# A hybrid convolution and retention layer on one core: an early pool for the first pair, other engines and places for small steps

## The chip, the core and the metric

The kernel runs on one core of a Trainium2 chip. Its engines work side by side, each through its own row of instructions: TensorE (PE; its weight loads are PEld), VectorE (DVE), ScalarE (ACT), GpSimd (POOL) and SyncE (SP), which here issues most transfers. Transfers can also be issued from ScalarE's and GpSimd's rows. The metric is device time in microseconds, the median of several runs; lower is better. All data are fp32.

## The reference

One decoder layer for x of 1024 positions by 1024 channels. A conditioned RMS norm gives u; one projection gives the parts of a convolution branch (gated a, a causal depthwise convolution over 31 positions, a layer norm, a 1024 by 1024 product, a gate) and of a retention branch with 4 heads (q and k with a rotary turn, chunks, a head norm, a gate). Both go through one output projection, a gated residual and a last RMS norm.

```python
u = _rmsnorm(h, norm_g[l]) * (1.0 + scale) + shift
proj = u @ w_in[l]          # conv a, b, gate; q, k, v; ret gate
a = conv_a * jax.nn.sigmoid(conv_bp)
a = _causal_depthwise_conv(a, conv_w[l], conv_b[l])
a = jax.nn.silu(_layernorm(a, conv_ln_g[l], conv_ln_b[l]))
y_conv = (a @ conv_pw[l]) * jax.nn.silu(conv_gate)
r = _retention_chunkwise(_rotary(q), _rotary(k) * RET_QK_DIM ** -0.5, v)
y_ret = _head_groupnorm(r, ...) * jax.nn.silu(ret_gate)
h = h + gate * (jnp.concatenate([y_conv, y_ret], axis=-1) @ w_out[l])
return _rmsnorm(h, final_g)
```

## The kernel before

**Three matmuls for one.** Every fp32 operand is split into a high part (a cast on ScalarE) and a low part (the operand less its high part, on VectorE or GpSimd); `split` (L69 to 71) does both, and `mm3` (L81 to 84) multiplies high by high, low by high and high by low. A low part is an instruction with two operands in SBUF.

**Stages in order of time.** `head` (L145 to 258) norms and turns x and projects the first four units of 128 output channels (tiles ps_e, ps_pcc, ps_paa, ps_pdd), step by step over eight blocks of the inner dimension; `make_u` (L206) gives uh and ul of a block, `mod` (L193, tile junk) the conditioning, `wel` (L166) the weights' low part. At its end the weights of the two *plain* units (22 and 23) are split (`hi_s`, `lo_s`, L256). Then the plain units run (L330), and beside them the sums of quarters of u for the pairs (L317 to 319, tile xs) and their splits th and tl.

**Pairs.** The other projection units go two by two, 21 pairs, each with seven block products in place of eight: blocks 11, 12, 21, 22 of a pair's weights are loaded (tiles pr), added and subtracted on GpSimd (s1 to s4; tiles sm and pr, L383), and split (ph on ScalarE L377, pl on GpSimd L378). `operands` (L368) does this, `pair` (L455) multiplies into the PSUM tiles pa, pd and pb. While a pair runs, VectorE does the convolution's taps of earlier channels (`conv_taps`, L260): 30 instructions at L271 for each of eight groups of 128 channels, in PSUM (yp) or, for the last group, in SBUF (y). At the end of each group GpSimd adds it to ysum (L278).

**Values, retention and norm.** The first half of the values (tiles ps_v, vs; L498 to 517) follows the pairs. `retention` (L585) then does heads 0 to 3, four chunks each (a tile of head 2, chunk 1 has 21 in its name): loads of q, k, sg, v, their splits (qch, qcl, kch, kcl, vch, vcl), scores sp, sm, outputs op and ob, the state, a norm (rs on GpSimd, nb on VectorE, rn on ScalarE, tp on TensorE), and a store of the gated result to d_yr (L691). `values` (L574) does the second half of the values among heads 0 and 1. `ln_squares` (L535) takes the mean over channels with two matmuls of ysum (tiles mu, negmu), subtracts it from eight loaded groups (ys, L546), stores these again and adds up their squares (L553). `ln_scale` (L555) makes the scale from that sum, `norm_z` the normed groups, `pointwise` (L714) the 1024 by 1024 product.

**Output.** `load_r` (L741) loads and splits blocks of the output weights (wo, woh, wol), which are multiplied with the stored halves d_yr and d_yc.

**What sets the order.** A scheduler writes each engine's row ahead of time from the order of the program, its priorities and modelled times; on the chip an engine takes its row in that order and waits where an operand isn't ready. Tiles come from pools; a place in a pool is used again when its last reader is done, and pools opened one after another take the memory of those closed before.

```python
        for tag, dt, bufs in (("raw", F32, 6), ("sum", F32, 3), ("ph", F32R, 7), ("pl", F32R, 7)):
            op_.tile([P, HK, P], dt, tag=tag, name=f"first_{tag}", bufs=bufs)
```

## Time and profile before

| | us |
|---|---|
| median of three runs | 982.46 (981.14 to 988.12) |
| profiled execution, its time | 983.87 |
| its span, first to last instruction | 982.1 |
| TensorE busy | 942.8 |
| VectorE busy | 742.7 |
| ScalarE busy | 410.4 |
| GpSimd busy | 395.6 |
| mean granted clock of TensorE | 0.984 |

Durations in the profile are those of the one profiled execution, and times in it count from the span's start. The granted clock is a share of full speed. An engine that shows little busy time can still be what another waits for; such waits stand in brackets in the timelines, with the instruction that ended them.

### The profile page before, as it was taken

The page shows a single profiled execution, that of the slowest core. Times are in us where ns is not written, and L with a number is a line of the kernel's source. Part 1 is how long each engine was busy: PE and PEld are TensorE (multiplying, and loading weights), DVE is VectorE, ACT ScalarE, POOL GpSimd, SP SyncE. Part 2 cuts the span into 40 slices and gives each one's busy share as a digit, 9 for nine tenths or more (in the row PEclk, how much of TensorE's full clock was granted, in tenths as well). Part 3 has the DMA queues.
Part 4 walks back from the last instruction along what each step waited for, and adds up shares of the span by engine and source line. Part 5 has one row for each costly group of instructions (what it writes and reads, how often), then busy time and mean ns, then how long its engine had stood idle before and what let it go on. Part 6 is the DMA issues. An engine that isn't in the chain of part 4 may idle for free.

```text
span 982.1 us, 12550 instructions
## 1 busy us (share of the span) xinstructions
PE 942.8 (96%) x4496; PEld 786.4 (80%) x4496; DVE 742.7 (76%) x926; ACT 410.4 (42%) x676; POOL 395.6 (40%) x356
## 2 busy tenths in 40 slices
PE   6999999999999999999999899979998999999996
PEld 5877788888888888888888788868887876888886
DVE  6989989898999999999799747788874354522322
ACT  7755543424334334343431556577543233311201
POOL 3021998878978878897561111212111000000000
PEclk9999999999999999999999899989999999999999
DMA  9912333324343334443344757875974386432111
GB/s 352 328 58 69 114 119 135 111 86 125 112 128 130 128 108 140 132 147 105 145 134 152 272 163 261 313 240 179 326 231 150 108 288 220 150 113 86 64 43 44
DMA packets 85441, 154.95 MB, mean 158 GB/s; under 512 B 6657, under 2 KB 44289, under 8 KB 84098
## 3 DMA queue, kind: packets, MB, share of 16 engines
q1 hardware_dynamic: 83074, 148.12, 44.9%
q10 hardware_dynamic: 1584, 3.41, 0.9%
q0 software_dynamic: 720, 2.62, 0.7%
q8 instruction: 35, 0.57, 0.2%
q14 instruction: 28, 0.23, 0.1%
HBM read 107.99 MB, written 46.14 MB: 157 GB/s over the span
## 4 chain that ended last, share of the span: by engine, by line
PE 79%; DMA 8%; DVE 5%; issue 3%; ACT 2%; POOL 1%; SPq 0%; POOLq 0%; DVEq 0%; ACTq 0%
PE pa L84 8%; PE pa L83 8%; PE pa L82 8%; PE ps_o L83 4%; PE ps_o L84 4%; PE ps_o L82 4%; PE pb L84 4%; PE pb L82 4%; PE pb L83 4%; DMA wo<-w_out 3%; PE ps_v L82 2%; PE ps_v L83 2%; PE ps_v L84 2%; PE pd L82 2%; PE pd L84 2%
## 5 line engine op out<-in xcount | busy, mean ns | idle before, releaser
L271 DVE SCALAR_TENSOR_TENSOR yp<-a,vec_t,yp 128x1024 f32<-128x1024 f32 x210 | 269.6, 1284 | 15.0 <-ACT yp L269 11.1
L378 POOL TENSOR_TENSOR pl<-pr,ph 128x512 fp32r<-128x512 f32 x63 | 83.8, 1336 | 70.9 <-ACT ph L377 70.5
L378 POOL TENSOR_TENSOR pl_s<-sm_s,ph_s 128x512 fp32r<-128x512 f32 x63 | 83.3, 1326 | 25.3 <-ACT ph_s L377 21.3
L675 POOL TENSOR_TENSOR rs<-mv,kc_t 128x2 f32<-128x2 f32 x16 | 6.3, 394 | 187.9 <-DVE mv L672 176.6
L377 ACT CAST ph_s<-sm_s 128x512 fp32r<-128x512 f32 x63 | 39.0, 622 | 99.9 <-PE pa L83 95.1
L790 POOL TENSOR_TENSOR fr<-fr,mhalf 128x1 f32<-128x1 f32 x7 | 3.8, 545 | 177.6 <-DVE fr L789 177.6
L377 ACT CAST ph<-pr 128x512 fp32r<-128x512 f32 x63 | 38.7, 621 | 75.9 <-PE pa L83 31.4
L82 PE MATMUL pa<-th,ph_s 128*128 128x512 f32 x168 | 65.5, 390 | 1.0 <-ACT ph_s L377 1.0
L84 PE MATMUL pa<-th,pl_s 128*128 128x512 f32 x168 | 65.5, 390 | 0.7 <-POOL pl_s L378 0.7
L82 PE MATMUL pb<-uh,ph_s 128*128 128x512 f32 x168 | 65.4, 389 | 0.0
L83 PE MATMUL pa<-tl,ph_s 128*128 128x512 f32 x168 | 65.4, 389 | 0.0
L83 PE MATMUL pb<-ul,ph_s 128*128 128x512 f32 x168 | 65.4, 389 | 0.0
L84 PE MATMUL pb<-uh,pl_s 128*128 128x512 f32 x168 | 65.4, 389 | 0.0
L383 POOL TENSOR_TENSOR sm_s<-pr,pr 128x512 f32<-128x512 f32 x42 | 55.7, 1326 | 5.2 <-PE pa L84 1.8
L83 PE MATMUL ps_pw<-zl,hi_pw 128*128 128x512 f32 x128 | 50.8, 397 | 1.1 <-DVE zl L71 1.1
L84 PE MATMUL ps_pw<-zh,lo_pw 128*128 128x512 f32 x128 | 50.3, 393 | 0.0
L271 DVE SCALAR_TENSOR_TENSOR y<-a,vec_t,y 128x1024 f32<-128x1024 f32 x30 | 44.4, 1480 | 6.6 <-ACT y L269 5.8
L82 PE MATMUL ps_pw<-zh,hi_pw 128*128 128x512 f32 x128 | 48.6, 404 | 0.0
L781 DVE TENSOR_TENSOR g<-ps_o,gate 128x512 f32<-128x512 f32 x14 | 9.5, 690 | 49.3 <-PE ps_o L84 49.3
L83 PE MATMUL ps_o<-wol,hi_yr 128*128 128x512 f32 x112 | 44.6, 398 | 0.1
L84 PE MATMUL ps_o<-woh,lo_yr 128*128 128x512 f32 x112 | 44.1, 396 | 0.0
L83 PE MATMUL ps_o<-wol,hi_yc 128*128 128x512 f32 x112 | 44.0, 393 | 0.1
(446 smaller groups left out, 2800.5 us busy)
## 6 DMA issues: line engine op xcount, KB each, us to landing
pr<-w_p SPq DMA_DIRECT2D x84, 256.0 KB, 2.8
aw<-ada_ss SPq DMA_DIRECT2D x8, 1024.0 KB, 7.5
d_qk<-ro SPq DMA_DIRECT2D x16, 512.0 KB, 3.3
wo<-w_out SPq DMA_DIRECT2D x16, 512.0 KB, 4.4
xt<-x SPq DMA_DIRECT2D x8, 512.0 KB, 6.8
d_sg<-o SPq DMA_DIRECT2D x16, 256.0 KB, 2.1
sg<-d_sg SPq DMA_DIRECT2D x16, 256.0 KB, 4.0
v<-d_v SPq DMA_DIRECT2D x16, 256.0 KB, 3.9
```

What stands on the lines that cost most here:

```text
L82: nc.tensor.matmul(ps, lh, rh, start=start, stop=False, skip_group_check=more)
L83: nc.tensor.matmul(ps, lh, rl, start=False, stop=False, skip_group_check=more)
L84: nc.tensor.matmul(ps, ll, rh, start=False, stop=stop, skip_group_check=more)
L271: nc.vector.scalar_tensor_tensor(acc, ap[:, j:j + S], col(V_CW, m * CW + j), acc, op0=MUL, op1=ADD)
L377: nc.scalar.copy(hi, src)
L378: nc.gpsimd.tensor_tensor(lo, src, hi.bitcast(F32), op=SUB)
L383: nc.gpsimd.tensor_tensor(out, a, b, op=op)
L675: nc.gpsimd.tensor_tensor(rs, mv[:, :, 1], kc_t[:, K_G2 + 2 * h:K_G2 + 2 * h + 2], op=MUL)
L781: nc.vector.tensor_tensor(g[:, :n], ps(), gate[:, sl], op=MUL)
L790: nc.gpsimd.tensor_tensor(r, r, mhalf[:, 0:1], op=ALU.pow)
```

## The change

Five things. The low parts of the plain units' weights are made on VectorE. A small pool, `early`, is opened ahead of the pool of th and tl, in memory that the head has used; the first pair's loads, the splits of its blocks 11 and 12 and its sums are written ahead of the plain units and live there, as the raw blocks of all pairs do; the parts of 11 and 12 get rings of two places, the others of five, where all shared rings of seven. `ln_squares` is written ahead of the second values of head 0 and no longer behind them. The stores of d_yr in the last head are issued from GpSimd's row. And the tags of the retention pool are placed in another order: mask, q, k, v, sg, vch and vcl first, ktl last.

```diff
@@ -253,7 +253,7 @@
         for j, n in enumerate(STD):
             hi = sw.tile([P, KT, P], F32R, tag="hi", name=f"hi_s{n}")
             lo = sw.tile([P, KT, P], F32R, tag="lo", name=f"lo_s{n}")
-            split(hi, lo, raw[:, j].rearrange("p (k c) -> p k c", k=KT), nc.gpsimd)
+            split(hi, lo, raw[:, j].rearrange("p (k c) -> p k c", k=KT))
             ws.append((hi, lo))
         return ps, ws
 
@@ -307,6 +307,10 @@
 
 
     one_ctx = ctx.enter_context(ExitStack())
+    early_p = one_ctx.enter_context(tc.tile_pool(name="early", bufs=1, reuse_waits="tile"))
+    pools = {"a": early_p}
+    for tag, dt, bufs in (("rawa", F32, 3), ("rawb", F32, 3), ("sum", F32, 3), ("pha", F32R, 2), ("pla", F32R, 2)):
+        early_p.tile([P, HK, P], dt, tag=tag, name=f"first_{tag}", bufs=bufs)
     tpool = one_ctx.enter_context(tc.tile_pool(name="t", bufs=1, reuse_waits="tile"))
     th = {i: tpool.tile([P, HK, HALF], F32R, name=f"th{i}") for i in (2, 3, 4)}
     tl = {i: tpool.tile([P, HK, HALF], F32R, name=f"tl{i}") for i in (2, 3, 4)}
@@ -321,6 +325,38 @@
         split(th[3][:, k], tl[3][:, k], x12)
         split(th[4][:, k], tl[4][:, k], x21)
 
+    def parts(pools, src, p, n):
+
+        tag, bufs = ("a", 2) if n in ("11", "12") else ("b", 5)
+        hi = pools[tag].tile([P, HK, P], F32R, tag="ph" + tag, name=f"ph{p}_{n}", bufs=bufs)
+        lo = pools[tag].tile([P, HK, P], F32R, tag="pl" + tag, name=f"pl{p}_{n}", bufs=bufs)
+        nc.scalar.copy(hi, src)
+        nc.gpsimd.tensor_tensor(lo, src, hi.bitcast(F32), op=SUB)
+        return hi, lo
+
+    def blocks(p, pools):
+
+        raw = {}
+        for i, b in enumerate(("11", "12", "21", "22")):
+            raw[b] = early_p.tile([P, HK, P], F32, tag="rawa" if i < 2 else "rawb", name=f"pr{p}_{b}", bufs=3)
+            nc.sync.dma_start(raw[b], w_p[p, i])
+
+        def sum_(n, a, b, op, out=None):
+            out = early_p.tile([P, HK, P], F32, tag="sum", name=f"sm{p}_{n}", bufs=3) if out is None else out
+            nc.gpsimd.tensor_tensor(out, a, b, op=op)
+            return out
+
+        o = {"11": parts(pools, raw["11"], p, "11"), "12": parts(pools, raw["12"], p, "12")}
+        s3 = sum_("s3", raw["11"], raw["21"], SUB)
+        s1 = sum_("s1", raw["21"], raw["22"], ADD, raw["21"])
+        s2 = sum_("s2", s1, raw["11"], SUB)
+        yield o, {"s2": s2, "s1": s1, "s3": s3, "22": raw["22"]}
+        s4 = sum_("s4", raw["12"], s2, SUB)
+        yield s4
+
+    first_blocks = blocks(0, pools)
+    first_parts = next(first_blocks)
+
     def gate_out(n, ps):
         cg = const.tile([P, S], F32, tag="sig", name=f"cg{n}")
         for i in range(2):
@@ -338,9 +374,19 @@
 
     with tc.tile_pool(name="one", bufs=1, reuse_waits="tile") as op_, \
             tc.tile_pool(name="oneps", bufs=1, space=bass.MemoryType.PSUM) as ops:
-
-        for tag, dt, bufs in (("raw", F32, 6), ("sum", F32, 3), ("ph", F32R, 7), ("pl", F32R, 7)):
-            op_.tile([P, HK, P], dt, tag=tag, name=f"first_{tag}", bufs=bufs)
+        pools["b"] = op_
+
+        def operands(p):
+            g = first_blocks if p == 0 else blocks(p, pools)
+            o, rest = first_parts if p == 0 else next(g)
+            if p == 0:
+                gate_out(n, ps)
+            for b in ("s2", "s1", "s3"):
+                o[b] = parts(pools, rest[b], p, b)
+            o["s4"] = parts(pools, next(g), p, "s4")
+            o["22"] = parts(pools, rest["22"], p, "22")
+            return o
+
         for m in range(2):
             conv_taps(m, a_early[m], ops)
 
@@ -364,38 +410,6 @@
             for k in range(HK):
                 rh, rl = mv(k)
                 mm3(ps, op[0][:, k], op[1][:, k], rh, rl, start and k == 0, k == HK - 1, not start or not stop)
-
-        def operands(p):
-            raw = {}
-            for i, b in enumerate(("11", "12", "21", "22")):
-                raw[b] = op_.tile([P, HK, P], F32, tag="raw", name=f"pr{p}_{b}", bufs=6)
-                nc.sync.dma_start(raw[b], w_p[p, i])
-
-            def parts(src, n):
-                hi = op_.tile([P, HK, P], F32R, tag="ph", name=f"ph{p}_{n}", bufs=7)
-                lo = op_.tile([P, HK, P], F32R, tag="pl", name=f"pl{p}_{n}", bufs=7)
-                nc.scalar.copy(hi, src)
-                nc.gpsimd.tensor_tensor(lo, src, hi.bitcast(F32), op=SUB)
-                return hi, lo
-
-            def sum_(n, a, b, op, out=None):
-                out = op_.tile([P, HK, P], F32, tag="sum", name=f"sm{p}_{n}", bufs=3) if out is None else out
-                nc.gpsimd.tensor_tensor(out, a, b, op=op)
-                return out
-
-            o = {"11": parts(raw["11"], "11"), "12": parts(raw["12"], "12")}
-            if p == 0:
-                gate_out(n, ps)
-            s3 = sum_("s3", raw["11"], raw["21"], SUB)
-            s1 = sum_("s1", raw["21"], raw["22"], ADD, raw["21"])
-            s2 = sum_("s2", s1, raw["11"], SUB)
-            o["s2"] = parts(s2, "s2")
-            o["s1"] = parts(s1, "s1")
-            o["s3"] = parts(s3, "s3")
-            s4 = sum_("s4", raw["12"], s2, SUB)
-            o["s4"] = parts(s4, "s4")
-            o["22"] = parts(raw["22"], "22")
-            return o
 
         sigs = {}
 
@@ -501,7 +515,7 @@
             split(uh[k][:, S2], ul[k][:, S2], x12)
         ws = []
         for k in range(KT):
-            raw = op_.tile([P, HALF], F32, tag="raw", name=f"wv0{k}", bufs=6)
+            raw = early_p.tile([P, HALF], F32, tag="raw" + "ab"[k % 2], name=f"wv0{k}", bufs=3)
             nc.sync.dma_start(raw, w_v[0, k // 2][:, k % 2])
             hi, lo = (t[:, k % HK] for t in ((th[2], tl[2]), (th[3], th[4]))[k // HK])
             split(hi, lo, raw, nc.gpsimd)
@@ -526,10 +540,12 @@
     with tc.tile_pool(name="ret", bufs=1, reuse_waits="tile") as rp, \
             tc.tile_pool(name="retps", bufs=1, space=bass.MemoryType.PSUM) as rps:
 
-        for tag, n, dt, bufs in (("vs", HALF, F32, 3), ("state", HALF, F32, 1), ("sth", HALF, F32R, 2),
+        for tag, n, dt, bufs in (("mask", 3 * P, F32, 1), ("q", HALF, F32, 2), ("k", HALF, F32, 2), ("v", HALF, F32, 2),
+                                 ("sg", HALF, F32, 2), ("vch", HALF, F32R, 2), ("vcl", HALF, F32R, 2),
+                                 ("vs", HALF, F32, 3), ("state", HALF, F32, 1), ("sth", HALF, F32R, 2),
                                  ("stl", HALF, F32R, 2), ("ob", HALF, F32, 2), ("rn", CH, F32, 2), ("yn", CH, F32, 2),
                                  ("sh", 3 * P, F32R, 2), ("sl", 3 * P, F32R, 2), ("sm", 3 * P, F32, 1),
-                                 ("gap", P, F32, 1)):
+                                 ("gap", P, F32, 1), ("ktl", HALF, F32R, 2)):
             rp.tile([P, n], dt, tag=tag, name=f"first_{tag}", bufs=bufs)
 
         def ln_squares():
@@ -688,7 +704,7 @@
                     nc.scalar.activation(yn, tp[:, d], AF.Identity, scale=col(V_GG, 2 * h + d),
                                          bias=col(V_GB, 2 * h + d))
                     nc.vector.tensor_tensor(sg[:, d], sg[:, d], yn, op=MUL)
-                nc.sync.dma_start(d_yr[2 * h:2 * h + 2, :, ts].rearrange("d p s -> p d s"), sg)
+                (nc.gpsimd if h == H - 1 else nc.sync).dma_start(d_yr[2 * h:2 * h + 2, :, ts].rearrange("d p s -> p d s"), sg)
 
         def norm_z(m):
             yt = fo.tile([P, S], F32, tag="yt", name=f"yt{m}", bufs=2)
@@ -703,10 +719,10 @@
         zh, zl = [None] * KT, [None] * KT
         for h in range(H):
             retention(h)
+            if h == 0:
+                ln_squares()
             if h < 2:
                 values(range(h * HK, (h + 1) * HK))
-            if h == 0:
-                ln_squares()
             if h == 1:
                 rbs = ln_scale()
                 for m in range(KT):
```

The three places below are from the rows that the scheduler wrote.

VectorE near the end of the head, before; xs are the sums of quarters, lo_s22 and lo_s23 (after) the plain units' low parts:

```order
L193 SCALAR_TENSOR_TENSOR junk_132,mod7_599<-aw7_591,cbc_130 128x1024
L318 TENSOR_TENSOR xs_123<-xs_123 128x512
L166 TENSOR_TENSOR wel6_556<-wer6_553,weh6_555 128x512
L193 SCALAR_TENSOR_TENSOR junk_132,mod7_599<-aw7_591,cbc_130 128x1024
L319 TENSOR_TENSOR xs_123<-xs_123 128x512
L206 TENSOR_TENSOR ul6_108<-xs_123,uh6_100 128x1024
```

And after:

```order
L193 SCALAR_TENSOR_TENSOR junk_132,mod7_599<-aw7_591,cbc_130 128x1024
L322 TENSOR_TENSOR xs_123<-xs_123 128x512
L166 TENSOR_TENSOR wel6_556<-wer6_553,weh6_555 128x512
L71 TENSOR_TENSOR lo_s22_634<-raw_s_631,hi_s22_633 128x1024
L193 SCALAR_TENSOR_TENSOR junk_132,mod7_599<-aw7_591,cbc_130 128x1024
L323 TENSOR_TENSOR xs_123<-xs_123 128x512
L71 TENSOR_TENSOR lo_s23_638<-raw_s_631,hi_s23_637 128x1024
L206 TENSOR_TENSOR ul6_108<-xs_123,uh6_100 128x1024
```

The two low parts have come in ahead of ul6, one on each side of junk and xs.

TensorE where the first values end, before; ps_v07 is the last of them, names in 00 belong to the first chunk of head 0:

```order
L84 MATMUL ps_v07_4578<-th3_663,ul7_109 128x512
L617 MATMUL kp00_4652<-ident_t_76,k00_4640 128x128 x2
L82 MATMUL sp00_4669<-qch00_4665,kch00_4661 128x256
L83 MATMUL sp00_4669<-qcl00_4666,kch00_4661 128x256
L84 MATMUL sp00_4669<-qch00_4665,kcl00_4662 128x256
```

After:

```order
L84 MATMUL ps_v07_4582<-th3_671,ul7_109 128x512
L557 MATMUL mu0_5096<-ysum_85,ones_t_78 128x512
L557 MATMUL mu1_5099<-ysum_85,ones_t_78 128x512
L633 MATMUL kp00_4665<-ident_t_76,k00_4653 128x128 x2
L82 MATMUL sp00_4682<-qch00_4678,kch00_4674 128x256
```

ScalarE at the same place, before:

```order
L514 COPY vs04_4497<-ps_v05_4524 128x512
L70 CAST vch00_4646<-v00_4644 128x512
L70 CAST qch00_4665<-q00_4638 128x512
L70 CAST kch00_4661<-k00_4640 128x512
L620 ACTIVATE kth00_4650<-kp00_4652,kc_t_77 128x256
```

After:

```order
L528 COPY vs04_4501<-ps_v05_4528 128x512
L558 ACTIVATE negmu_5095<-mu0_5096 128x512
L558 ACTIVATE negmu_5095<-mu1_5099 128x512
L70 CAST vch00_4659<-v00_4657 128x512
L70 CAST qch00_4678<-q00_4651 128x512
L70 CAST kch00_4674<-k00_4653 128x512
L636 ACTIVATE kth00_4663<-kp00_4665,kc_t_77 128x256
```

The two matmuls of the mean and both negmu now stand ahead of the first chunk's casts, transposes and scores.

SP's row ahead of the output weights, before; d_yc and cgl belong to the pointwise product, sg33 is the last chunk of the last head:

```order
L721 DMA d_yc_69<-cgl5_7204 128x1024
L717 DMA cgl7_7326<-d_cg_67 128x1024
L721 DMA d_yc_69<-cgl6_7265 128x1024
L691 DMA d_yr_68<-sg33_6746 128x2x256
L774 DMA h10_7627<-x 128x1024
L743 DMA wo8_7331<-w_out 128x1024
L743 DMA wo9_7337<-w_out 128x1024
L754 DMA fgt_7379<-final_g 128x1024
```

After:

```order
L737 DMA d_yc_69<-cgl5_7217 128x1024
L733 DMA cgl7_7339<-d_cg_67 128x1024
L759 DMA wo8_7344<-w_out 128x1024
L759 DMA wo9_7350<-w_out 128x1024
L770 DMA fgt_7392<-final_g 128x1024
L737 DMA d_yc_69<-cgl6_7278 128x1024
L759 DMA wo10_7356<-w_out 128x1024
```

The store of sg33 is gone from this row, and wo8 and wo9 have passed d_yc of cgl6.

## Rows read from the trace of the kernel before

**Rows 1.** The page's first part: busy time of each engine.
```profile
PE 942.8 (96%) x4496; PEld 786.4 (80%) x4496; DVE 742.7 (76%) x926; ACT 410.4 (42%) x676; POOL 395.6 (40%) x356
```

**Rows 2.** Windows; us, busy us (instructions) of each engine, granted clock, DMA share.
```profile
...
92.00:105.00 13.00, 9.37 (x37) 6.24 (x36) 12.68 (x12) 6.78 (x13) 10.20 (x9) 1.00 0.63 202
105.00:535.00 430.00, 430.00 (x1898) 356.10 (x1897) 406.35 (x395) 165.12 (x277) 328.46 (x247) 1.00 0.38 124
541.00:555.00 14.00, 11.09 (x60) 9.99 (x59) 12.05 (x20) 7.97 (x14) 0.85 (x2) 0.76 0.86 298
555.00:625.00 70.00, 70.00 (x419) 61.52 (x418) 45.72 (x87) 40.15 (x71) 11.34 (x20) 1.00 0.66 223
625.00:655.00 30.00, 22.65 (x139) 20.42 (x138) 27.09 (x52) 22.77 (x37) 8.20 (x9) 0.83 0.91 318
743.00:750.00 7.00, 4.49 (x27) 4.28 (x26) 4.54 (x8) 4.60 (x8) 0.00 (x0) 0.76 0.69 218
800.00:830.00 30.00, 25.73 (x99) 18.68 (x98) 14.51 (x12) 12.48 (x12) 0.00 (x0) 0.94 0.80 261
```

**Rows 3.** Timelines, 53 to 62: start, us, line, what; brackets: idle before, releaser.
```profile
53.42 5.32 POOL L71 TENSOR_TENSOR lo_s<-raw_s,hi_s 128x1024 fp32r<-128x1024 f32 x2 [34.40 <-ACT hi_s L70]
53.59 2.90 DVE L166 TENSOR_TENSOR wel<-wer,weh 128x512 fp32r<-128x512 f32 x1
56.41 3.41 DVE L193 SCALAR_TENSOR_TENSOR junk<-aw,cbc 128x1024 bf16<-128x1024 f32 x1
...
61.62 0.50 PE L83 MATMUL ps_e<-ul,weh 128*128 128x512 f32 x1 [2.41 <-DVE ul L206]
```

**Rows 4.** Timeline of VectorE: the tl splits.
```profile
72.09 7.31 DVE L71 TENSOR_TENSOR tl<-xs,th 128x512 fp32r<-128x512 f32 x12
```

**Rows 5.** Groups of VectorE by line and shape: busy us, mean ns, idle before.
```profile
L546 DVE TENSOR_TENSOR ys<-ys,negmu 128x1024 f32<-128x1024 f32 x8 | 9.7, 1218 | 10.4 <-DMA ys<-d_y 5.6 <-ACT negmu L542 4.8
L71 DVE TENSOR_TENSOR lo_pw<-raw_pw,hi_pw 128x1024 fp32r<-128x1024 f32 x8 | 9.6, 1216 | 1.5 <-ACT hi_pw L70 1.5
L553 DVE TENSOR_TENSOR ysum<-ysum,sq 128x1024 f32<-128x1024 f32 x7 | 8.4, 1207 | 0.0
```

**Rows 6.** Timeline of TensorE behind the plain units.
```profile
94.49 0.50 PE L82 MATMUL pa<-uh,ph 128*128 128x512 f32 x1 [1.70 <-ACT ph L377]
```

**Rows 7.** Timelines of ScalarE and VectorE: change of tap group, last taps.
```profile
486.76 0.60 ACT L444 ACTIVATE o<-pa 128x512 f32<-128x512 f32 x1 [1.97 <-PE pa L84]
...
524.86 13.17 DVE L271 SCALAR_TENSOR_TENSOR y<-a,vec_t,y 128x1024 f32<-128x1024 f32 x10
```

**Rows 8.** Timelines of GpSimd, TensorE and ScalarE: the sum, the mean, its negative.
```profile
538.87 2.41 POOL L278 TENSOR_TENSOR ysum<-ysum,y 128x1024 f32<-128x1024 f32 x1
...
588.73 1.02 PE L541 MATMUL mu<-ysum,ones_t 128*128 128x512 f32 x2
...
590.76 0.60 ACT L542 ACTIVATE negmu<-mu 128x512 f32<-128x512 f32 x1 [0.19 <-PE mu L541]
```

**Rows 9.** Timeline of TensorE, second chunk of head 0.
```profile
546.44 0.55 PE L82 MATMUL sp<-qch,kch 128*128 128x256 f32 x1 [1.05 <-DVE sm L634]
```

**Rows 10.** Timeline of TensorE between heads 1 and 2.
```profile
647.97 0.69 PE L617 MATMUL kp<-ident_t,k 128*128 128x128 f32 x2 [2.55 <-DVE state L660]
```

**Rows 11.** TensorE at 746; chain of waits ahead of it (start, us, what).
```profile
746.61 0.69 PE L685 MATMUL tp<-ident_t,rn 128*128 128x128 f32 x2 [2.52 <-ACT rn L683]
...
736.46 3.06 DMA d_yr<-sg
...
739.95 4.48 DMA k<-d_qk
```

**Rows 12.** Timelines of SP's queue and TensorE near the output stage.
```profile
770.04 0.33 SPq L717 DMA_DIRECT2D cgl<-d_cg  x1
783.17 0.91 SPq L743 DMA_DIRECT2D wo<-w_out  x2
...
807.21 1.54 PE L82 MATMUL ps_o<-woh,hi_yr 128*128 128x512 f32 x4 [2.02 <-ACT woh L70]
```

## Prediction

> **What bounds the kernel now.** Read the page's first part before anything else: TensorE is busy 942.8 of 982.1 us [rows 1]. The change adds and removes no matmul, so it can only give back TensorE's idle time and the time at a low granted clock, and nothing on another engine counts unless TensorE waits for it. Then the windows by stage, where the reader is to look at PE against the width and at PEclk: from 105 to 535 us TensorE has no gap [rows 2], so neither the pairs nor VectorE's taps under them hold the end; the same is true of 555 to 625. The loss stands in a few short stretches: 3.63 us in 92 to 105, 2.91 in 541 to 555, 7.35 in 625 to 655, 2.51 in 743 to 750, 4.27 in 800 to 830 [rows 2], and one wait of 2.41 at 61.6 [rows 3]. In four of them the granted clock is below 1.00. [...] Each time the fall stands in a stretch where TensorE waited. [...] The timeline of each stretch then names who was waited for.
>
> **The change part by part**, against the profiled execution's own 983.87; the median of the runs is 1.41 below that.
>
> A. Low parts of the plain units to VectorE. Before, two 1024-wide instructions on GpSimd (5.32 us) lie beside VectorE's wel and junk, which take 2.90 and 3.41 us, where the same sizes take 0.61 (7.31 by 12, the tl splits [rows 4]) and 1.22 [rows 5]; ul6 comes late and TensorE waits 2.41 for it [rows 3]. So two engines that each read both operands from SBUF hold one another up here. After, the two low parts cost VectorE 1.216 each, the price of the same subtraction elsewhere [rows 5], 2.4 in all, and 2.29+2.19 = 4.5 of blocking goes: VectorE is 2.1 us ahead at ul6, and so is TensorE, which waited longer than that. -2.1; bounds -2.4 and 0 (VectorE is late for another reason).
>
> [...]
>
> B. The first pair early. Between the plain units and the pair's third product TensorE loses 3.63 us in four waits, the first 1.70 for ScalarE's cast of block 11 [rows 2, 6]: its raw block had no place until the head's memory was free and the new pool was open. After, loads, casts and the five GpSimd steps stand among the plain units' work, 96 matmuls at 0.2266 (430.00 by 1898 [rows 2]), 21.8 us of TensorE, enough for a load, a cast and a chain of five steps of 1.3. -3.6, bounds -3.64 and 0 (the places are not free any sooner).
>
> C. The norm's squares ahead of the second values. The order puts two matmuls of the mean right behind the last first-half value, and both negmu ahead of the casts of v, q and k for the first chunk. Who is queued behind the wait: on TensorE all of head 0, on ScalarE those three casts, which before had been done under the values. With A and B TensorE gets there at 541.0-5.7 = 535.3. The sum over channels needs the last tap. Taps begin behind the tl splits (72.09+7.31 [rows 4]) and are 2.1 earlier with A; at the change to the last group VectorE waits for ScalarE's start of y, and ScalarE for 1.97 us for a product of the last pair ahead of it [rows 7], which goes with an earlier TensorE. The last tap, at 524.86+13.17 = 538.03 before [rows 7], so ends near 534.0. The sum over channels was there at 538.87+2.41 = 541.28 [rows 8], 3.25 behind it: now 537.2, a wait of 1.9. From the first mu to the end of the second negmu it took 2.63 [rows 8]; three casts follow, each of negmu's size (0.60 [rows 8]), and two low parts of 0.61: the first chunk's scores flow at 537.2+2.63+1.8+1.2 = 542.8. Of the 5.6 from 537.2, TensorE has about 2 of work (the mean, the transposes, the scores' first matmul), so some 3.6 are idle; 1.05 at the second chunk [rows 9] stay. 1.9+3.6+1.05 = 6.6 in place of 2.9: **+3.7**, bounds 0 (the sum is in time and the casts hide under the mean) and +8 (ends 4 later, or the clock falls once more).
>
> D. 625 to 655. Here the squares' 18.1 us of VectorE [rows 5] lie in the row with the second head's work: VectorE is busy 27.1 of 30, DMA 0.91 [rows 2], and TensorE waits for its results, 2.55 for state among them [rows 10]. Idle 7.35 and clock 5.1 make 12.4. After, the squares, 16 transfers of 512 KB among them, are done before this stretch, while the variance, the scale and the pointwise loads stay. I keep a third: **-8.3**, bounds -12.4 and 0.
>
> E. 744. TensorE waits 2.52 for rn; the chain behind it runs through the load of k for the last chunk, issued at 739.95, and SP got to that load only behind stores of head output that waited for their data (the chain passes from one at 736.46 to it) [rows 11]. The stores go to GpSimd's queue and SP passes. With half of 3.41 us at the lower clock (0.76 of 7 us) the stretch is worth 4.2; I take -3.5, since k still stands behind one such store, that of the third head's last chunk: bounds -4.2 and 0. On GpSimd the store waits for VectorE's product, and the next chunk's rs is queued behind it: 0.54 of issue at most on a chain with idle on both sides, costed at nothing, +1 if it shows.
>
> F. The output weights. The first late weight was issued at 783.17, behind stores that wait; in the new order it follows cgl7, which issued at 770.04 [rows 12]. TensorE idles 4.27 in 800 to 830, the first wait 2.02 for woh, at clock 0.94 (1.7 us) [rows 2, 12]. All the waits of the stretch are shorter together than the 13.1 us of earlier issue, so none would be left if each weight's place in memory were free as early; places come free as TensorE uses the weights up, and some of the lead is lost there. -3.9, two thirds of 5.9; bounds -5.9 and 0.
>
> G. What moved to 535 to 605. VectorE had 45.7 of 70 there, DMA 0.66 [rows 2]: 18.1 us of squares and 8 MB fit by sum, but in-order queues make the pieces wait. By the rate of idle at the busiest stretch (7.35 in 30 us) over the 30 us in which they fall, +7 and a little clock; by the present stretch, 0. I take +3, nearer the present rows; bounds 0 and +8.
>
> Sum: -2.1-3.6+3.7-8.3-3.5-3.9+3.0 = -14.7; 983.87-14.7 = 969.2, less 1.4, at the median **968**.
>
> **The rivals.**
> R1. The hold moves to the taps. Two low parts and four sums, six GpSimd instructions of 1.33 (5.32 by 4 for half the width), fall beside the twelve tl splits (7.31 us together). In rows 3 VectorE lost 4.5 to 5.32 of GpSimd: of 8.0 here that is 6.7. The taps end that much later, and the matmuls of the mean, now in TensorE's row, wait for them; 967.8+6.7 = 974.5. For it: rows 3 show the mechanism. Against: the six need their loads and ScalarE's casts first, so only some fall beside the splits.
> R2. The squares choke the first head as they did the second: G takes what D gives. 967.8+8.3 = 976.1. For it: 2.9 of idle in 541 to 555 already, DMA at 0.86; against: 555 to 625 has none, with VectorE at 65%.
> R3, slower. SP issues in order, and eight stores of centred channels that wait for VectorE now stand between the k, q and v loads of head 0. If the 70 us run as 625 to 655 did (12.4 lost per 30), that is 28.9; 967.8-3.0+28.9 = 993.7. It decides for slower from a loss of 17.7 in that stretch. For it: E shows exactly this hold in the queue; against: before, too, the squares began behind the mean at 588.73 [rows 8], among the first head's loads, and TensorE has no gap up to 625 [rows 2].
> R4. The small pool does nothing: its places lie over tiles that TensorE reads till the head's end. B is lost (+3.6), and C shrinks by its wait of 1.9: 969.5.
>
> **How the numbers follow.** About 1% (972.6, 992.3) is what a measurement of this kernel tells from no change. Forecast 0.54 (0.49 below 972.6), R1 0.12 (0.04), R2 0.18 (0.03), R4 0.07 (0.06), R3 0.09. Faster 0.62, same 0.29, slower 0.09. With A, D and F at their good ends the time is 967.8-0.3-4.1-2.0 = 961.4, and with C and G halfway to theirs (3.4) 958; with C and G at their bad ends it is 967.8+4.3+5.0 = 977.1, and R2 with a bad C gives 980.4. Range 957 to 980: about 0.05 lies below, 0.05 above and R3's 0.09 beyond it.
>
> **What would show it.** Right: wel and junk at 0.7 and 1.2 near 54 us; no wait between the plain units and pa; a TensorE gap of some 5 to 7 us right behind the first values, ended by mu and then by a cast or its low part; a row without gaps around the variance matmuls; no gap at tp before the output stage; woh ahead of need. Wrong: long tl splits and taps that end late (R1); gaps for ktl or qcl all through head 0 (R2); k or q loads issued behind d_y stores, PEclk under 0.9 there (R3); a cast of block 11 that still ends TensorE's wait (R4). The forecast is most exposed at D, the largest term, of which I keep two thirds by judgement, and at C, where an earlier TensorE only meets the taps sooner.

## The result, and the profile after

The changed kernel takes **968.97 us** in the median of four runs (966.86 to 970.08), against 982.4 for the kernel before: a ratio of 0.985 (0.9808 to 0.9891), so 1.5% faster. 968 was forecast. The profiled execution has a span of 968.3. Most of the terms were not what was forecast, and they made up for each other: that the total came out within a microsecond is luck.

The page's first part, where the reader is to see that TensorE runs as many matmuls as before [rows 1], with less idle time, and with 5.6 us less of busy time, most of it because less lies at the lower clock (mean 0.988, before 0.984, a loss of 11.6 us for 15.7):

```profile
PE 937.2 (97%) x4496; PEld 784.5 (81%) x4496; DVE 745.3 (77%) x928; ACT 412.2 (43%) x676; POOL 389.8 (40%) x358
```

Windows of the changed kernel by stage (columns as in [rows 2]); each but that of 650 to 700 answers to one of [rows 2], some four microseconds earlier at first and ten at the end:

```profile
89.00:101.00 12.00, 12.00 (x55) 9.94 (x54) 11.75 (x11) 7.30 (x12) 8.89 (x8) 1.00 0.21 74
534.00:549.00 15.00, 10.27 (x47) 8.05 (x46) 10.35 (x16) 9.26 (x16) 2.57 (x2) 0.80 0.63 234
549.00:626.00 77.00, 77.00 (x474) 68.68 (x472) 55.25 (x102) 46.84 (x80) 10.69 (x24) 0.99 0.83 283
626.00:650.00 24.00, 18.45 (x117) 16.84 (x116) 19.98 (x48) 18.25 (x32) 3.25 (x5) 0.79 0.55 177
650.00:700.00 50.00, 45.39 (x270) 38.86 (x271) 41.39 (x71) 36.68 (x58) 7.91 (x16) 1.00 0.65 216
740.00:747.00 7.00, 7.00 (x39) 5.99 (x38) 3.31 (x10) 2.26 (x4) 1.32 (x4) 1.00 0.22 75
790.00:825.00 35.00, 34.79 (x149) 27.29 (x147) 18.04 (x16) 13.56 (x14) 0.00 (x0) 1.00 0.76 247
```

TensorE's idle time is the width less PE; the loss of clock is the share that PEclk lacks of 1.00, times the width.

| stage | before | after | measured | forecast |
|---|---|---|---|---|
| A, wait for ul | 2.41 | 0.35 | -2.1 | -2.1 |
| B, first pair | 3.63 | 0.00 | -3.6 | -3.6 |
| C, start of head 0 (idle) | 2.9 | 4.7 | +1.8 | +3.7 |
| G, rest of head 0 | 0.00 | 0.00 | 0 | +3.0 |
| D, 625 to 655, idle and clock | 12.4 | 10.6 | -1.8 | -8.3 |
| the 50 us behind D (idle) | 1.1 | 4.6 | +3.5 | none |
| E, near 744 | 4.2 | 0.00 | -4.2 | -3.5 |
| F, output weights | 5.9 | 0.2 | -5.7 | -3.9 |

For the sixth row the 50 us of before are 655 to 705, where TensorE was busy 48.88. The terms measured sum to -12.1; the span fell by 13.8. The other 1.7 belong to no term. By the places of the same matmuls in the two timelines, the last matmul of the values' first half comes 6.3 us earlier (540.70 and 534.38), where A and B make 5.7; the first matmul of the output 7.6 earlier (790.99 and 783.39), where the terms make 6.4; and 0.4 lies in the output and behind it. The clock in the head, where the kernel before has 1.7 of loss and the changed kernel none, gave nothing, of which more at the end.

The head, VectorE and TensorE. To be seen: wel and junk have the length that their size has elsewhere, with the low parts (one of two is shown) between them, where [rows 3] had 2.90 and 3.41:

```profile
53.87 0.69 DVE L166 TENSOR_TENSOR wel<-wer,weh 128x512 fp32r<-128x512 f32 x1
54.47 1.22 DVE L71 TENSOR_TENSOR lo_s<-raw_s,hi_s 128x1024 fp32r<-128x1024 f32 x1
55.60 1.22 DVE L193 SCALAR_TENSOR_TENSOR junk<-aw,cbc 128x1024 bf16<-128x1024 f32 x1
...
59.77 0.50 PE L83 MATMUL ps_e<-ul,weh 128*128 128x512 f32 x1 [0.35 <-DVE ul L206]
```

The first pair. Its loads go out at 63.50 (93.23 before), and GpSimd works beside the last splits; the last two lines show both engines slower where they meet: 1.74, where the same instruction of GpSimd takes 1.29 at 69.98, and 1.78 for the 0.61 of [rows 4]. The taps begin at 77.70, before at 79.31:

```profile
63.50 16.39 SPq L342 DMA_DIRECT2D pr<-w_p  x7
...
72.93 1.74 POOL L334 TENSOR_TENSOR pl<-pr,ph 128x512 fp32r<-128x512 f32 x1
71.74 1.78 DVE L323 TENSOR_TENSOR xs<-xs 128x512 f32<-128x512 f32 x1
```

The start of head 0, where [rows 7] and [rows 8] stood. TensorE waits 1.35 for the sum over channels, runs the mean, and waits 2.01 for the cast of k, which stands third behind the second negmu on ScalarE:

```profile
536.13 1.98 PE L557 MATMUL mu<-ysum,ones_t 128*128 128x512 f32 x4 [1.35 <-POOL ysum L278]
540.34 0.38 PE L82 MATMUL sp<-qch,kch 128*128 128x256 f32 x1 [2.01 <-ACT kch L70]
...
538.15 0.60 ACT L558 ACTIVATE negmu<-mu 128x512 f32<-128x512 f32 x1 [0.26 <-PE mu L557]
```

The wait for the cast isn't all new: at the same place the kernel before waited for the low part qcl.

```profile
543.08 0.38 PE L83 MATMUL sp<-qcl,kch 128*128 128x256 f32 x1 [1.64 <-DVE qcl L71]
```

Between the heads. The variance begins at 620.92, nine microseconds ahead of the 630.25 of before (last line); but its last columns follow at 627.77, behind a transpose that TensorE waits for, VectorE's rstd comes at 631.27, behind steps of the second head in its row, and the matmuls of the scale (rb) begin at 638.85, where they began at 636.56 before. The lead is lost in the rows. From 626 to the first product (ps_pw, 650.22) TensorE waits eight times, the longest for sth, a cast of the second head; seven of the waits are for the second head's steps on ScalarE and VectorE, and only the last, 0.73, for a normed group (zh). In the 50 us behind, 3.2 of the 4.6 of idle are for normed groups, where it was 1.07 before:

```profile
620.92 1.17 PE L574 MATMUL var<-ones_t,ysum 128*128 128x1 f32 x10
638.85 1.11 PE L584 MATMUL rb<-rs_d,ones_t 128*128 128x128 f32 x8
...
631.27 0.16 DVE L576 TENSOR_SCALAR rstd<-var 128x8 f32<-128x8 f32 x1
...
629.35 0.58 PE L82 MATMUL op<-sth,qch 128*128 128x256 f32 x1 [1.30 <-ACT sth L70]
670.12 0.50 PE L83 MATMUL ps_pw<-zl,hi_pw 128*128 128x512 f32 x1 [2.19 <-DVE zl L71]
...
630.25 1.95 PE L558 MATMUL var<-ones_t,ysum 128*128 128x1 f32 x16 [0.34 <-DVE ysum L553]
```

The queue of SP near the end, for [rows 11] and [rows 12]: k for the last chunk at 727.42 and the first late weights 18.4 us ahead of the output's first matmul (783.4); before, 7.8 ahead:

```profile
727.42 0.53 SPq L619 DMA_DIRECT2D k<-d_qk  x1
765.04 0.90 SPq L759 DMA_DIRECT2D wo<-w_out  x2
```

### The profile page after: what moved, and what is told of

Its sections match the earlier page's. It is cut to its first block, busy times and chain, and to the rows that moved or that the text cites. A ratio compares the mean times of both kernels' runs of the same rounds, so it can differ in the third digit from the quotient of the medians.

```text
span 968.3 us, 12531 instructions
## 1 busy us (share of the span) xinstructions
PE 937.2 (97%) x4496; PEld 784.5 (81%) x4496; DVE 745.3 (77%) x928; ACT 412.2 (43%) x676; POOL 389.8 (40%) x358
## 3 DMA queue, kind: packets, MB, share of 16 engines
q10 hardware_dynamic: 1584, 3.41, 0.9%
## 4 chain that ended last, share of the span: by engine, by line
PE 78%; DVE 10%; DMA 5%; issue 3%; ACT 2%; POOL 1%; POOLq 0%; DVEq 0%; ACTq 0%
PE pa L83 7%; PE pa L84 7%; PE pa L82 7%; DVE y L271 4%; PE ps_o L83 4%; PE ps_o L84 4%; PE ps_o L82 4%; PE pb L83 4%; PE pb L82 4%; PE pb L84 4%; PE ps_pw L82 2%; PE ps_pw L84 2%; PE ps_pw L83 2%; DMA wo<-w_out 2%; PE pd L84 2%
## 5 line engine op out<-in xcount | busy, mean ns | idle before, releaser
L334 POOL TENSOR_TENSOR pl_s<-sm_s,ph_s 128x512 fp32r<-128x512 f32 x63 | 85.4, 1356 | 36.6 <-ACT ph_s L333 35.1
L84 PE MATMUL ps_o<-woh,lo_yc 128*128 128x512 f32 x112 | 43.6, 390 | 0.0
```

Source lines behind the costliest of these rows:

```text
L84: nc.tensor.matmul(ps, ll, rh, start=False, stop=stop, skip_group_check=more)
L334: nc.gpsimd.tensor_tensor(lo, src, hi.bitcast(F32), op=SUB)
```

## The experiments

They ran in three other jobs, where the kernel before took 987.77, 987.43 and 985.76 us, so ratios to it are what compares, and places are compared within the profiles. Line numbers differ by a few between kernels. An edit also lets the scheduler write other rows, so a stage can change that the edit doesn't touch. Each kernel has one profile, and the changed kernel two.

**The low parts on GpSimd again.**

```diff
-            split(hi, lo, raw[:, j].rearrange("p (k c) -> p k c", k=KT))
+            split(hi, lo, raw[:, j].rearrange("p (k c) -> p k c", k=KT), nc.gpsimd)
```

> The changed kernel with one part undone: the plain units' low parts on GpSimd again. Changed kernel for comparison: 968.97. If the hold between two engines that both read SBUF cost the 2.41 us wait of before, it comes back: VectorE instructions near 54 us of 2.5 us and more, a TensorE wait for ul of 2 to 2.4 in place of 0.35, and 970.5 to 971.5. Rival: the wait came from VectorE's row being full, and the two low parts on it cost as much as they saved; then the wait for ul stays under 0.5 and the time within 0.5 of 969.

Ratio 0.9827 (0.9796 to 0.9859), 970.13 us. Timelines of VectorE and TensorE in this kernel:

```profile
53.52 2.89 DVE L166 TENSOR_TENSOR wel<-wer,weh 128x512 fp32r<-128x512 f32 x1
56.32 3.41 DVE L193 SCALAR_TENSOR_TENSOR junk<-aw,cbc 128x1024 bf16<-128x1024 f32 x1
...
61.54 0.50 PE L83 MATMUL ps_e<-ul,weh 128*128 128x512 f32 x1 [2.38 <-DVE ul L206]
```

The hold is back to within 0.03 of [rows 3], and so is the wait: A is shown. The time of the whole doesn't show 2 us: this profile had 2.3 less idle in 650 to 735.

**The first pair written late, its small pool kept.**

```diff
-    first_blocks = blocks(0, pools)
-    first_parts = next(first_blocks)
...
-            g = first_blocks if p == 0 else blocks(p, pools)
-            o, rest = first_parts if p == 0 else next(g)
+            g = blocks(p, pools)
+            o, rest = next(g)
```

> The changed kernel with the first pair's loads, parts and sums written in their old place, behind the plain units; the small pool and the rings stay. If writing them early is what gave the 3.64 us, four TensorE waits of about that sum come back between the plain units and the pair, less up to 1.35 since TensorE then meets the last sum over channels later: 971 to 973. Rival: the place in memory was enough, the scheduler moves the loads ahead by itself, and the waits stay away: 969.

Ratio 0.9803 (0.977 to 0.9836), 968.77 us: the rival. A window of this kernel behind the plain units, and its first loads:

```profile
89.00:101.00 12.00, 12.00 (x54) 9.94 (x54) 11.75 (x10) 7.29 (x12) 9.21 (x8) 1.00 0.18 67
...
63.18 16.44 SPq L342 DMA_DIRECT2D pr<-w_p  x7
```

The scheduler sends the loads at 63.18 where they are written late, too. So the small pool, with its place in memory that the head has freed, is enough to give B.

**The squares late again.**

```diff
-            if h == 0:
-                ln_squares()
             if h < 2:
                 values(range(h * HK, (h + 1) * HK))
+            if h == 0:
+                ln_squares()
```

> The changed kernel with the norm's squares behind the second values again, as before. By the prediction's terms (C +3.7, D -8.3, G +3.0) the early squares are a gain of 1.6, so this run is 1.6 slower, 970.5, with waits of 7 us and more between the first and second head. By what the trace of the changed kernel shows (C cost 1.8, the stretch between the heads still loses 5.8 of idle, and waits for the normed groups behind it are new, 4.1 against 1.1), the early squares are a loss of some 3, so this run is faster, 965 to 967. Rival: neither, the scheduler makes another row of the rest and the time is within 1 of 969.

Ratio 0.9873 (0.9847 to 0.9899), 975.52 us: slower, but not for either reason given. Windows of this kernel from the end of the first head's values to the output:

```profile
620.00:650.00 30.00, 23.51 (x141) 21.16 (x140) 27.02 (x52) 22.71 (x37) 8.20 (x9) 0.83 0.93 321
650.00:700.00 50.00, 48.38 (x284) 41.79 (x283) 42.75 (x74) 33.24 (x52) 8.94 (x16) 1.00 0.71 233
785.00:825.00 40.00, 34.31 (x135) 25.25 (x134) 18.10 (x15) 15.41 (x15) 0.00 (x0) 0.96 0.75 246
```

The stretch between the heads is that of before (6.5 idle, 0.83), 1 us off the changed kernel's; the 50 us behind it lose 1.6 and not 4.6, as the trace reading had it. At the start of head 0 TensorE still waits 1.85 for qcl and 1.15 for sm, so that what the early squares cost there is little more than the wait for the sum. What decides is the last line: 5.7 of idle for the output weights are back, at 0.96, though the last head's stores still go by GpSimd.

**The last head's stores on SP again.**

```diff
-                (nc.gpsimd if h == H - 1 else nc.sync).dma_start(d_yr[...], sg)
+                nc.sync.dma_start(d_yr[...], sg)
```

> The changed kernel with the last head's stores issued from SP again. In its row the load of k for the last chunk stays ahead of those stores, and the first late output weights stand behind the last of them. If such a store holds the queue, the weights issue when its product is ready, TensorE waits for woh come back (4.2 of idle and 1.7 of clock before) and the time is 973 to 975, while the wait at 744 (2.52) stays away. Rival: the last head is done so much sooner against the pointwise product that no store waits; then 969.

Ratio 0.9823 (0.979 to 0.9855), 970.7 us: the rival, nearly. In 735 to 760 TensorE was busy 25.00 of 25. A window at the output weights:

```profile
790.00:830.00 40.00, 38.80 (x161) 29.33 (x160) 19.86 (x20) 15.67 (x15) 0.00 (x0) 1.00 0.68 215
```

That is 1.2 of idle, where the changed kernel's first profile had 0.2 and its second, below, 1.1. So with all else changed no cost of the stores on SP is shown.

**The early squares alone**, on the kernel before: the diff of u_squares_late the other way round.

> The kernel before with one part alone: the norm's squares written ahead of the second values. By the prediction's terms the stretch between the first and second head loses 4 us in place of 12.4, the start of head 0 costs 3.7 more and the rest of it 3: 982 for the profiled run. By what the changed kernel's trace and the run without early squares show, the stretch between the heads keeps 10 to 12 us of idle and clock loss, head 0 has none, the start costs 2, and the output weights, which the scheduler then puts ahead of a store of the pointwise product, are no longer waited for (up to 5.9 back), less 1 to 3 for waits on the normed groups: 979 to 982. The total hardly tells the two apart, the stretches do.

Ratio 0.9882 (0.9853 to 0.9912), 975.53 us, better than by either reading. Windows of the stretch between the heads and behind it, of the place of 744 and of the output weights:

```profile
632.00:656.00 24.00, 19.22 (x132) 16.81 (x131) 20.98 (x45) 20.01 (x35) 4.37 (x5) 0.93 0.65 213
656.00:700.00 44.00, 40.35 (x241) 35.13 (x240) 35.80 (x66) 32.19 (x51) 9.30 (x16) 0.96 0.65 206
740.00:765.00 25.00, 25.00 (x143) 21.83 (x142) 10.29 (x23) 7.83 (x15) 1.32 (x4) 1.00 0.40 131
795.00:835.00 40.00, 39.93 (x167) 30.51 (x166) 20.18 (x19) 16.14 (x16) 0.00 (x0) 1.00 0.71 230
```

So this part by itself ends both E and F, with all stores on SP. It shortens the stretch between the heads to 4.8 of idle and 1.7 of clock (0.93), from 12.4 together, but 3.7 and 1.8 lie behind it, where before 1.1 did: of D's price, 1.5 is gained in all.

**The stores on GpSimd alone**, on the kernel before: the diff of u_dyr_sp the other way round.

> The kernel before with one part alone: the last head's stores issued from GpSimd. The load of k for the last chunk then has only stores of the head before ahead of it, so the TensorE wait of 2.52 near 744 and its clock (1.7) go: 979.5 to 980 for the profiled run. The prediction also gave the output weights' waits (4.2 and 1.7) to this part; since the weights here still stand behind a store of the pointwise product (issued at 779 before), I now expect those waits to stay, 3 or more; if they go, 974, and the stores of the last head were their cause.

Ratio 0.9948 (0.9927 to 0.9968), 982.7 us. Windows at 744 and at the output weights:

```profile
735.00:760.00 25.00, 25.00 (x150) 21.95 (x149) 12.34 (x28) 10.59 (x20) 3.42 (x9) 1.00 0.46 147
795.00:825.00 30.00, 25.61 (x99) 18.53 (x98) 14.52 (x12) 12.38 (x12) 0.00 (x0) 0.94 0.79 253
```

E goes (25.00 of 25); F stays, 4.4 idle at 0.94. The prediction gave F in part to these stores, and moved alone they do nothing for it.

**Two weights' loads by another queue**, on the kernel before.

```diff
-            nc.sync.dma_start(raw, w_out[f])
+            (nc.gpsimd if f in (KT, KT + 1) else nc.sync).dma_start(raw, w_out[f])
```

> The kernel before with an edit that the change doesn't have: the loads of the first two late output weights go out from GpSimd's row, which has nothing left to wait for there; all else stays. If SP's row held them (stores that wait ahead of them), they issue ten microseconds earlier, at 770 to 775, and the waits for woh in 800 to 830 (4.2 and 1.7 of clock) shrink to 2 or less: 978 to 980. If their place in memory held them until the last head's tiles were read, they issue at 781 or later as before and the waits stay: 984.

Ratio 0.999 (0.9971 to 1.0008). The loads went out at 778.00, five microseconds earlier than in [rows 12] and 14.1 ahead of the output's first matmul, between the two cases named; the waits stayed, with 4.6 of idle at 0.94 in 800 to 830:

```profile
778.00 1.17 POOL L743 DMA_DIRECT2D wo<-w_out  x2 [2.56 <-issue]
```

TensorE's first wait (2.82) comes 14.4 us into the output, past the two weights that were moved. So the issue of the first two alone is not the lever. Two things go with the waits over the runs: how far the last head ends ahead of the output (from the end of TensorE's last transposes tp to the first matmul of the output, ps_o), and how far ahead of the output the load of the third late weight goes out (negative: behind it). The idle time is TensorE's in 781 to 930:

| kernel | last tp to ps_o | third weight ahead | idle |
|---|---|---|---|
| before | 10.7 | 0.9 | 4.3 |
| stores alone | 10.7 | -0.2 | 4.4 |
| two weights by GpSimd | 10.7 | 0.0 | 4.6 |
| squares late | 10.5 | -0.1 | 5.7 |
| early squares alone | 15.3 | 6.7 | 0.1 |
| stores on SP | 15.8 | 6.4 | 1.2 |
| low parts on GpSimd | 15.7 | 8.8 | 0.5 |
| pair late | 15.8 | 8.8 | 0.1 |
| tags in the old order | 15.8 | 8.8 | 0.0 |
| after | 15.8 | 8.8 | 0.2 |
| after, once more | 15.8 | 8.8 | 1.1 |
| negative on VectorE | 15.8 | 8.8 | 1.1 |

**The scale ahead of the second head's values**, on the changed kernel, with the edit of b_wo_pool.

```diff
+            if h == 1:
+                rbs = ln_scale()
             if h < 2:
                 values(range(h * HK, (h + 1) * HK))
             if h == 1:
-                rbs = ln_scale()
                 for m in range(KT):
```

> The changed kernel with the norm's variance and scale written ahead of the second head's values, and the first two late output weights loaded from GpSimd's row. The changed kernel's stretch from 626 to 650 loses 5.6 of idle and 5.1 of clock though VectorE and the transfers have room there. If that is for want of other matmuls beside a chain of steps of the second head and the norm (the values end at 621, the pointwise product begins at 650), the values now lie under the chain and the stretch loses under 4: 961 to 965. Rival: the chain's steps on VectorE and ScalarE are the limit, and values in between only lengthen them; the loss moves with the chain and the time is 968 to 973.

Ratio 0.9968 (0.9951 to 0.9985), 984.29 us: slower than either case named. Windows of the chain of variance and scale, of the 55 us behind it, and of the output's start:

```profile
586.00:604.00 18.00, 14.81 (x88) 14.23 (x87) 13.72 (x30) 9.66 (x19) 1.64 (x1) 0.72 0.89 312
604.00:659.00 55.00, 55.00 (x329) 48.24 (x328) 37.86 (x68) 37.59 (x60) 6.46 (x16) 1.00 0.57 183
780.00:802.00 22.00, 8.38 (x29) 6.16 (x28) 6.85 (x8) 5.64 (x6) 1.90 (x3) 0.69 0.85 274
...
781.14 0.77 POOL L707 DMA_DIRECT2D d_yr<-sg  x1 [8.41 <-DVE sg L706]
```

With values among the chain of the scale TensorE has no gap from 604 to 659, where the changed kernel's 626 to 659 has eight; but 3.2 of idle and 5.0 of clock stand at the chain's start instead, so most of the loss moved with the chain, as the rival had it. From the end of the first head to 735 it loses 10.6 in all, with 2.3 of idle behind 659, against the changed kernel's 15.2 (5.8 and 4.3 of idle, 5.1 of clock), or 13.7 in its second profile. Then the output waits 12.9 for its weights at 0.69. Here the last head ends at 778.7, eleven later, and the first late weight goes out at 781.91, from GpSimd's row, behind a store of the last head that waited 8.41 for its product (last line). So the weights' queue, the second edit of this run, took part in that loss, and the run doesn't price the moved scale by itself.

**The changed kernel once more.**

> The changed kernel itself once more, to stand beside the others of this job on the same chip and to show which of its losses come again. Expected: 0.983 to 0.987 of the kernel before; no wait for ul over 0.5 near 59, none at the pair, none at 744, none for woh; 4 to 5 us of idle in 535 to 560, 5 to 6 in 620 to 655, 2 to 5 in 655 to 735; the stretches at half clock in the head and near 650 come and go.

Ratio 0.9826 (0.9799 to 0.9854), 969.12 us, span 967.3. As expected but for two places: the start of head 0 has 3.75 of idle (2.95 of it in 535 to 560), where the first profile had 4.73, and there is 1.06 of idle for woh at 817. Between the heads 6.1 of idle come again, at 3.4 of clock and not 5.1; behind 655, 4.2.

**The mean's negative on VectorE**, on the changed kernel.

```diff
-                nc.scalar.mul(negmu[:, sl], mu, -1.0 / D)
+                nc.vector.tensor_scalar(negmu[:, sl], mu, -1.0 / D, None, op0=MUL)
```

> The changed kernel with the mean's negative made on VectorE, so that ScalarE's casts of the first chunk don't stand behind it. If those casts were what TensorE waited for (2.01), they are done under the values and that wait goes; the low parts on VectorE now stand behind the negative, two instructions of 0.7, so a wait of up to 1.5 for qcl takes its place: a net gain of 0.5 to 2 in 535 to 560, 967 to 968.5. Rival: the wait for the sum over channels grows to fill it, and nothing changes.

Ratio 0.9819 (0.9791 to 0.9847), 968.27 us, not to be told from 0.9826 beside it. TensorE at the start of head 0:

```profile
538.82 0.38 PE L83 MATMUL sp<-qcl,kch 128*128 128x256 f32 x1 [1.65 <-DVE qcl L71]
```

The wait for the cast went, so it was ScalarE's row that TensorE waited for. One of 1.65 for qcl, behind the two negatives in VectorE's row, took its place, as long as the one of the kernel before (1.64).

**The retention pool's tags in the old order.**

```diff
-        for tag, n, dt, bufs in (("mask", 3 * P, F32, 1), ("q", HALF, F32, 2), ("k", HALF, F32, 2), ("v", HALF, F32, 2),
-                                 ("sg", HALF, F32, 2), ("vch", HALF, F32R, 2), ("vcl", HALF, F32R, 2),
-                                 ("vs", HALF, F32, 3),
+        for tag, n, dt, bufs in (("vs", HALF, F32, 3),
...
-                                 ("gap", P, F32, 1), ("ktl", HALF, F32R, 2)):
+                                 ("gap", P, F32, 1)):
```

> The changed kernel with the retention pool's tags in their old order, the one part not yet taken alone. In the changed kernel the loads of the first chunks go out at 504 to 522, under the last values. If the new order of places gives them their memory, they go out later here and TensorE waits longer at the start of head 0, by 1 to 3 us: 970 to 972. Rival: the places are free either way, since everything that lay there is read by then; 969.

Ratio 0.9884 (0.9845 to 0.9923), 974.27 us; the loads go out at 535 where the changed kernel had them at 512 and the kernel before, without the small pool, at 516, and TensorE waits 4.57 for k, more than expected:

```profile
535.89 0.59 SPq L617 DMA_DIRECT2D q<-d_qk  x1
...
542.46 0.66 PE L631 MATMUL kp<-ident_t,k 128*128 128x128 f32 x2 [4.57 <-DMA k<-d_qk]
```

## Why the prediction was right, point by point

**A and B** were right in mechanism and in size. Of B, the run with the pair written late shows that the place does it. The prediction named the place as the cause and the writing as the cure; the second was not needed.

**R1** is there and small. VectorE's sums and splits beside GpSimd lose about 2.3 us (two steps of 1.78 for 0.61), a third of the 6.7 that the rival gave, and the taps still began 1.6 earlier, since the splits had started early, at 60.83, among VectorE's other steps. The run with the low parts on GpSimd shows the hold again, at 2.89 and 3.41 beside 5.28 us of GpSimd, where the changed kernel has 0.69 and 1.22; what in the two engines makes it, no run shows.

**C** was right in its mechanism, waits for the sum and then for the casts behind negmu, as the run with the negative on VectorE shows; its size was +1.8, not +3.7, and +0.8 in the changed kernel's second profile. The wait for the sum measured 1.35 for 1.9. Of the step from the sum to the flowing scores the prediction had 3.6 idle; 2.2 was measured (2.01 and 0.22), since the low parts ran beside the casts and not behind them. And a wait of 1.64 for qcl went away in its place, so that the wait for the sum is most of C's price.

**D failed**, and it was the largest term. The prediction's step was "the squares' 18.1 us of VectorE lie in the row with the second head's work", so that moving them gives back two thirds. The squares did go and VectorE is busy 19.98 of 24 there, and yet the stretch loses 10.6 where it lost 12.4. What the runs show instead: between the end of the values (621) and the pointwise product (650) TensorE has little but the steps of the second head and of the scale, and waits for the second head's, one after another. With values laid among them TensorE has no gap there, but 8.2 of loss move to the chain's start, and 4.6 of 15.2 come back in all (the run with the scale ahead; 3.1 against the second profile).

The nine microseconds by which the variance came earlier were lost in VectorE's and TensorE's rows, where its steps stand between those of the head. What in the rows of VectorE and ScalarE makes the head's steps late was not tried: the low part stl, for one, began right behind a low part of the pointwise weights of 1.21. Behind the stretch the product begins when it did (650.2 for 649.5), with the scale 2.3 later than before, and meets normed groups that are not ready: +3.5, of which about 2 are for these groups and 0.9 for a state, a stall for which the prediction had no term. Its cause was not tried apart. Nearly half of D's price was clock, 5.1 before (0.17 of 30 us [rows 2]) and 5.0 after, 3.4 in the second profile. In steps of 0.5 and 1 us the lower clock reads 0.50 in the traces of both kernels (634 to 637, 649 to 654 and, for E, 746.5 to 749.5 before; 629 to 638 after). In the run of early squares alone D's loss by it was 1.7, and 1.8 behind; whether the waits bring the clock down, and which of them, stays open. Nor does its loss follow their length: 541 to 555 has 2.91 of idle and 3.4 of clock [rows 2], and the changed kernel's 650 to 700 has 4.6 of idle at 1.00.

**G** was nothing, for the forecast's +3.0, and **R2** and **R3** did not come: 16 more transfers among the loads, DMA 0.83, VectorE 55.25 of 77, and TensorE 77.00 of 77. (R3's loss of 17.7 only takes back the whole gain; by the prediction's own 992.3, slower would take 27.5.)

**E** was right in size; the queue was its cause, as the stores alone show. But the early squares alone end it too: the scheduler then puts k (at 733.12) ahead of the store that held it.

**F** was under-sized and in part given to the wrong stores: "behind stores that wait". That the late weights go out too late is borne out, from the third on: 0.9 us ahead of the output or less in every kernel that waits over 4, 6.4 or more in the others. But the last head's stores can stay on SP (1.2), and moved alone they change nothing (4.4). The early squares do it: in every kernel with them but the one whose scale was moved, the last head ends 15.3 to 15.8 us ahead of the output, in every one without, 10.5 to 10.7. Why the head's matmuls then stand earlier among the pointwise product's is in the scheduler's model, and was not tried apart; nor was the weights' issue without the earlier end of the head.

**The tags** had no term. They undo a cost that comes with the small pool: with the pool and the old order the first loads of head 0 go out at 535, without the pool at 516, and about 5 us are lost. That the loads wait for places to come free is the reading of these two; no run shows the places. The cost was not in the sum on either side, and with the change as a whole it nets to nothing.

**R4** is ruled out by the loads at 63.50.

So the sum came to -14.7 for the wrong reasons in two large terms: D gave 6.5 less and what lies behind it cost 3.5, C and G together gave 4.9 back, F and E 2.5, and 1.7 lies in no term.

## What to carry to other kernels

Before a stall is put down to the engine that is busy in it, ask what work TensorE could do there at all: where only a chain of small steps is left, taking load off the other engines returned little here (1.8 of 12.4), and independent matmuls laid among the steps closed the gaps but moved most of the loss to the chain's start (8.2 there, for 15.2 in all before). Where a scheduler writes the rows, a part's gain can show far from its edit, so undo each part alone and read every stage, not only the one it was meant for. With a new pool ahead of others, look for loads that go out later (here at 535 for 516), and try giving these the places that come free first (here 512).

## What had not been expected of the hardware

TensorE's lower clock in the head came and went between two profiles of one kernel with the same rows (1.00 and 0.83 in 20 to 30 us), and cost nothing, by the places of the instructions behind it. The window of 20 to 30 us in the changed kernel, first profile and second, then a wait of TensorE behind it, which only the first has, and VectorE's wel of the second:

```profile
20.00:30.00 10.00, 9.08 (x50) 7.36 (x50) 9.97 (x18) 8.02 (x13) 0.00 (x0) 1.00 0.97 345
...
20.00:30.00 10.00, 9.23 (x42) 7.57 (x42) 9.97 (x17) 7.54 (x12) 0.00 (x0) 0.83 1.01 386
...
31.92 0.50 PE L83 MATMUL ps_e<-ul,weh 128*128 128x512 f32 x1 [0.73 <-DVE ul L206]
...
53.26 0.69 DVE L166 TENSOR_TENSOR wel<-wer,weh 128x512 fp32r<-128x512 f32 x1
```

At 0.83 over 10 us the loss is 1.7 us, and TensorE has 42 matmuls in the window for 50. Yet wel begins at 53.26 in the profile that lost them and at 53.87 in the one that didn't; in the kernel before, at 0.83 as well, it begins at 53.59 [rows 3]. VectorE is busy 9.97 of 10 in this window, and the TensorE that runs at the full clock waits for it instead. A lower clock did count in the kernel with the early squares alone: it came right behind the wait for ul, at 61.47, and the same stretch of the head's products took 17.9 us (52.25 to 70.11), where the kernel before took 16.3 (52.48 to 68.82) with nearly the same wait (2.49 and 2.41). So here a lower clock is priced by where the next stage begins, and not by the share alone.
